# A language-and-state trunk on one core: modulation weights by 256 features a load, the last block's prompt windows first, and its output projection in two column parts

## The chip, the cores and the metric

The kernel runs on one core of a Trainium2 chip. The metric is device microseconds of one execution; three executions took 3923.26, 3939.91 and 3950.05 us, median 3939.91. One further execution was profiled and took 3942.07 us. The engines are TensorE (PE in the profile, its weight loads apart as PEld), VectorE (DVE), ScalarE (ACT), GpSimd (POOL) and SyncE (SP), whose queue issues most DMAs in order.

## The reference, cut to what matters

One inference step of a two-layer trunk over 1152 tokens of 1024 features: a prompt of 1024 tokens and eight samples of 16 tokens. Layer 0 is an RWKV-7 time mixing, layer 1 a band attention; each is followed by a SwiGLU feed-forward block.

```
mod = silu(c) @ w_ada[l] + b_ada[l]           # (rows, 6 * 1024): shift, scale, gate, twice
h = rms_norm(x) * (1 + scale) + shift
... r, w, k, v, a, g = projections of mixes of h and its previous row
s = s * w_t + (s a_t) b_t + v_t k_t           # the state, 64 x 64 per head, token by token
y_t = s r_t
out = (norm(y) + bonus) * g @ w_o             # output projection
x = x + gate * out
x = x + gate_f * swiglu(h_f)                  # h_f from rms_norm(x), modulated
```

c has nine rows: one for the prompt and one for each sample. `silu(c) @ w` over both layers and the shared keys and values has 14336 output features; this product is the modulation.

## The kernel before

The tokens are cut into three blocks of 384 columns (features stand on the partitions). Blocks 0 and 1 are prompt; in block 2 columns 0 to 255 are prompt and 256 to 383 are the samples. A float32 gemm is three products in a faster float32 form, with each operand split in a high and a low part: `split` lets ScalarE copy (L255) and VectorE subtract (L256), `mm3` issues the products (all matmuls have line L139).

**Modulation.** `ada_steps` (L195) is a generator over units of 512 output features; there are 28. A unit has four loads of 512 KB. Before, a load holds two k tiles of 128 input features by 512 output features. The product with k tile 4h+q goes into PSUM rows 32q to 32q+31; the two halves h of a unit accumulate, and a yield stands between them. At the unit's end ScalarE copies the bank, four small matmuls add the four row groups and transpose, and VectorE adds the bias into `mod`. Other code advances the generator: `step` (L190) in `proj_h` (units 0 to 3, into tiles of the window pool), in `proj_v` of block 2 (L631), in `layer0a` for what is left of units 4 to 11, and in `begin` (L1334) of the first feed-forward block's down projection for units 12 to 27. In `layer0a`'s last part the loads go into the ring of tiles called `raw`, which has two buffers there and serves the weights of the output projection (`wunit`, L245) too; in the down projection they go into tiles called `h`.

**Windows.** The recurrence runs in nine windows of 128 columns, each in two halves of eight heads (hf 0 and 1), so that a unit 2w+hf stands for one window and half. `windows` (L1083) prepares a unit (`win_prep`: reads, Gram products G, transposes), runs its states (`win_state`) and, beside the next unit's run, closes the one before (`win_post`, which writes `yg`). Units 12 and 13 are window 6, units 14 and 15 window 7; both are prompt columns of block 2, and a half's window 7 needs its state from window 6. Units 16 and 17 are window 8, the samples, whose states come from the input.

**Output projection.** `outproj` (L1114) reads `yg` of a block (`mr`, split into 16 `mx` tiles), then for each of eight features loads and splits a weight of `rw_o`, runs 24 products, adds the gated residual (`residual`, L1104), writes `x1` and sums squares; at the end it writes the inverse norm `rr`. The feed-forward block's first token half (tokens 0 to 511) needs blocks 0 and 1 only, its second half needs block 2.

**What sets the order.** `alternate(a, b, m, n)` (L1056) takes m steps of one generator, then n of the other; so the program order is a mix of windows, modulation and projections. The framework's scheduler then orders each engine's instructions, with waits where data or a buffer is not ready; each engine, and SP's queue, runs its list in order. In `layer0a` (L1140) windows 6 to 8 run in the order 12 13 16 14 15 17, five steps to two of `early`: what is left of the modulation units, then `outproj(0)` and `outproj(1)`. After the windows the pool is closed, `outproj(2)` follows, and `dense` starts the feed-forward block in the memory that was freed.

Of the kernel before, what the change touches and what calls it, by code (L numbers as in the profile page):

```python
# [11 lines left out]
ALU = mybir.AluOpType  # L12
# [5 lines left out]
TB = 384  # L18
# [59 lines left out]
def prep(i):  # L78
    i = {k: np.asarray(v) for k, v in i.items()}
    d = {}  # L80
# [57 lines left out]
def mm(nc, out, lhsT, rhs, start, stop):  # L138
    return nc.tensor.matmul(out, lhsT, rhs, start=start, stop=stop)  # L139


class Trunk:
# [52 lines left out]
    def ada_steps(self, units, tag="aux", bufs=1, tile=None):  # L195

        nc = self.nc
        for u in units:
            ps = self.bank(tag, bufs)
            for h in range(2):  # L200
                w = [(tile or self.rawtile)() for _ in range(2)]
                for i in range(2):
                    nc.sync.dma_start(w[i][:, :1024], self.a["wada"][u, 2 * h + i])
# [12 lines left out]
            nc.vector.tensor_tensor(self.mod[:, u * 4:u * 4 + 4, :], pv, bv, ALU.add)  # L216
            yield
# [69 lines left out]
    def sq_done(self, st):  # L287

        w = st.acc.shape[-1]
        if w == TB:  # L290
            ss = self.bank("aux", 1)[:, :TB]
            parts = [(ss, 0, TB)]
# [100 lines left out]
    def proj_h(self, b):  # L393
# [15 lines left out]
        for f in range(8):  # L409
            x = hb[:, f]  # L410
            if b == 0:
                if f % 4 == 0:
                    self.step(4)
                nc.vector.tensor_scalar(self.A0[f], self.mod[:, 8 + f, :], 1.0, self.P("nm0", f), ALU.add, ALU.mult)
# [689 lines left out]
    def residual(self, n, f, gate, out, x, ps):  # L1104

        nc = self.nc
        nc.vector.scalar_tensor_tensor(out[:, :n], ps[:, :n], self.mod[:, gate + f, 0:1], x[:, :n], ALU.mult, ALU.add)  # L1107
        if n < out.shape[-1]:
# [4 lines left out]

    def outproj(self, b):  # L1114

        nc, pp = self.nc, self.pp
        cols = slice(b * TB, (b + 1) * TB)
        hi, lo = [], []
        for f in range(8):
            h, l = self.mtile(), self.mtile()  # L1120
            t = self.mraw()
            nc.sync.dma_start(t, self.yg[b][:, f, :])
            self.split(h, l, t)
            hi.append(h)
            lo.append(l)
        st = self.sq_open()
        for f in range(8):
            W = self.wunit(pp, self.a["rw_o"][f])
            pz = self.bank("acc", 2)
            self.gemm(pz[:, :TB], W, hi, lo)  # L1130
            x = self.ev("rr")
            nc.sync.dma_start(x, self.a["x"][b][:, f, :])
            o = self.ev("e0")
            self.residual(256 if b == 2 else TB, f, 16, o, x, pz[:, :TB])
            nc.sync.dma_start(self.x1[:, f, cols], o)
            self.sq_add(st, o)
            yield
        nc.sync.dma_start(self.rr[:, cols], self.sq_done(st))

    def layer0a(self, ctx):  # L1140
# [26 lines left out]
        for _ in self.outproj(2):  # L1167
            pass
# [150 lines left out]
    def ffn(self, l, B, W, part1, xsrc, dst, done):  # L1319
# [14 lines left out]
        def begin(p):  # L1334
# [6 lines left out]
            W[p] = [self.halves(self.a[f"wd{l}"][f]) for f in (2 * p, 2 * p + 1)]  # L1341
            self.step(3)

# [567 lines left out]
```

## Time and profile before

| what | us |
|---|---|
| median of three executions | 3939.91 |
| profiled execution, its span | 3942.07, 3940.1 |
| PE busy over the span | 3559.0 (90%) |
| VectorE, ScalarE, GpSimd busy | 2265.0, 1574.5, 712.4 |
| mean granted PE clock | 0.929 of full |
| first and last modulation load of the windows' end | 954.8 to 1077.4 |
| first matmul of `outproj(2)` | 1334.74 |
| first product of the feed-forward block | about 1394 |

The parts of a page: busy shares by engine, the span in 40 slices, DMA queues, the chain of work that ended last, and groups of instructions by line. A row of a group reads: line, engine, operation, out<-in, shape, count | busy us, mean ns of one | idle us before them, with what ended it. Rows of the timeline and of the chain begin with the start and the length in us. A float32 matmul that is not in the faster form shows as two records. Each engine's busy time is a union over its own instructions, and matmuls are pipelined, so the distance from start to start says more than a record's length.

### The profile page before, as it was taken

What the parts mean: (1) busy time and instruction counts of PE and PEld (TensorE: products, weight loads), DVE (VectorE), ACT (ScalarE), POOL (GpSimd) and SP (SyncE); (2) the same over time, 40 slices, a digit from 0 to 9 for tenths busy, and PEclk for the clock granted to TensorE, in tenths of its full rate; (3) what the DMA queues carried; (4) which work ended last, traced back from release to release, by engine and by line L of the source; (5) the groups of instructions that cost most, each with busy time, mean ns of one, the idle gap of its engine ahead of it and who ended that gap; (6) DMA issues with size and microseconds to landing.
All of it is one profiled execution on the core that took longest, in us unless ns stands there. A gap on an engine that the chain in (4) does not pass through costs nothing.

```text
span 3940.1 us, 71465 instructions
## 1 busy us (share of the span) xinstructions
PE 3559.0 (90%) x28172; PEld 3107.7 (79%) x28172; DVE 2265.0 (57%) x4238; ACT 1574.5 (40%) x2967; POOL 712.4 (18%) x635
## 2 busy tenths in 40 slices
PE   6878988888798789999999999888889799999999
PEld 4766776776386579999877778777777789999998
DVE  5475575474355665555456752466676665455567
ACT  5554565363233343333311253455554443333310
POOL 0110110020000254545100210100000265454000
PEclk8888998799689689999999999999999899999999
DMA  6785675667665322222654313255464422222522
GB/s 214 210 243 155 181 232 168 170 186 215 186 167 163 100 90 78 74 76 72 228 183 164 133 60 102 79 169 153 143 195 155 154 70 75 75 73 93 170 79 74
DMA packets 434720, 552.27 MB, mean 140 GB/s; under 512 B 128336, under 2 KB 300496, under 8 KB 429904
## 3 DMA queue, kind: packets, MB, share of 16 engines
q1 hardware_dynamic: 380240, 528.82, 43.0%
q10 hardware_dynamic: 54144, 18.89, 2.1%
q8 instruction: 222, 3.64, 0.4%
q14 instruction: 114, 0.93, 0.1%
HBM read 413.44 MB, written 134.12 MB: 139 GB/s over the span
## 4 chain that ended last, share of the span: by engine, by line
PE 61%; DMA 6%; DVE 5%; ACT 3%; POOL 2%; issue 1%; SPq 0%; ACTq 0%; DVEq 0%; POOLq 0%
PE S L139 31%; PE PT L139 15%; PE acc L139 7%; PE st L139 2%; PE O L139 2%; DVE h L256 1%; PE PT L1737 1%; PE aux L139 1%; PE Y L139 1%; PE G L139 1%; DMA raw<-in_wada 1%; ACT pts L1738 1%; DMA h<-qT 0%; DMA h<-out_kT 0%; DMA h<-in_wq 0%
## 5 line engine op out<-in xcount | busy, mean ns | idle before, releaser
L139 PE MATMUL S<-h,w 128*128 128x320 f32 (+1 forms) x4944 | 695.5, 300 | 16.1 <-DVE h L256 3.4
L139 PEld LDWEIGHTS S<-h,w 128*128 128x128 f32 x4944 | 674.6, 192 | 24.2 <-DVE h L256 7.8
L139 PE MATMUL acc<-mx,whi 128*128 128x384 f32 x1728 | 525.6, 383 | 49.2 <-ACT mx L255 20.2
L139 PE MATMUL S<-h,wh 128*128 128x320 f32 (+1 forms) x2844 | 532.6, 338 | 14.5 <-DVE h L1107 8.1
L139 PEld LDWEIGHTS S<-h,wh 128*128 128x128 f32 x2844 | 457.3, 190 | 83.4 <-DVE h L1363 15.8
L139 PEld LDWEIGHTS acc<-mx,whi 128*128 128x128 f32 x1728 | 355.7, 214 | 77.6 <-ACT mx L255 23.3
L255 ACT ACTIVATE w<-rq 128x512 fp32r<-128x512 f32 x308 | 191.9, 629 | 503.3 <-PE S L139 200.5
L256 DVE TENSOR_TENSOR w<-rq,w 128x512 fp32r<-128x512 f32 x308 | 268.3, 875 | 198.4 <-ACT w L255 196.9
L139 PE MATMUL PT<-h,w 128*128 128x320 f32 (+1 forms) x2448 | 353.4, 299 | 15.1 <-ACT w L255 6.9
L139 PEld LDWEIGHTS PT<-h,w 128*128 128x128 f32 x2448 | 336.0, 192 | 18.9 <-ACT w L255 7.3
L139 PE MATMUL acc<-mx,wlo 128*128 128x384 f32 x864 | 325.7, 377 | 2.4 <-DVE wlo L256 2.4
L139 PE MATMUL PT<-h,wh 128*128 128x320 f32 (+1 forms) x1428 | 286.1, 344 | 7.6 <-DVE wh L256 4.7
L1296 POOL TENSOR_TENSOR t<-t,t 128x576 f32<-128x576 f32 (+1 forms) x132 | 214.5, 1625 | 413.5 <-ACT t L1303 295.7
L139 PEld LDWEIGHTS PT<-h,wh 128*128 128x128 f32 x1428 | 234.3, 190 | 42.9 <-DVE h L1363 6.9
L139 PEld LDWEIGHTS acc<-mx,wlo 128*128 128x128 f32 x864 | 184.0, 213 | 10.0 <-DVE wlo L256 3.7
L256 DVE TENSOR_TENSOR wlo<-raw,whi 128x1024 fp32r<-128x1024 f32 x108 | 136.7, 1267 | 94.7 <-ACT whi L255 93.5
L255 ACT ACTIVATE wh<-rq 128x512 fp32r<-128x512 f32 x124 | 75.0, 626 | 259.6 <-PE S L139 156.2
L256 DVE TENSOR_TENSOR h<-h,h 128x1024 fp32r<-128x1024 f32 (+4 forms) x112 | 123.3, 1115 | 83.0 <-ACT h L255 67.8
L255 ACT ACTIVATE h<-h 128x1024 fp32r<-128x1024 f32 (+4 forms) x112 | 103.1, 934 | 157.5 <-DMA h<-sd 105.7
L1296 DVE TENSOR_TENSOR t<-S,t 128x576 f32<-128x576 f32 (+1 forms) x116 | 86.5, 745 | 135.5 <-PE S L139 135.5
L1363 DVE TENSOR_TENSOR h<-h,S 128x640 f32<-128x640 f32 (+1 forms) x150 | 112.0, 751 | 83.0 <-PE S L139 82.6
L255 ACT ACTIVATE whi<-raw 128x1024 fp32r<-128x1024 f32 x108 | 113.5, 1053 | 104.5 <-PE acc L139 78.9
(424 smaller groups left out, 5758.5 us busy)
## 6 DMA issues: line engine op xcount, KB each, us to landing
h<-in_wada SPq DMA_DIRECT2D x64, 512.0 KB, 5.8
rq<-in_wg SPq DMA_DIRECT2D x88, 256.0 KB, 2.6
rq<-in_wu SPq DMA_DIRECT2D x88, 256.0 KB, 2.6
rq<-in_wd SPq DMA_DIRECT2D x88, 256.0 KB, 2.9
raw<-in_wada SPq DMA_DIRECT2D x32, 512.0 KB, 4.5
kc<-in_ck SPq DMA_DIRECT2D x16, 1024.0 KB, 5.0
vc<-in_cv SPq DMA_DIRECT2D x16, 1024.0 KB, 5.7
sd<-t SPq DMA_DIRECT2D x88, 160.0 KB, 1.9
```

The costliest lines, as they stand in the source:

```text
L139: return nc.tensor.matmul(out, lhsT, rhs, start=start, stop=stop)
L255: self.nc.scalar.activation(hi, x, AF.Copy)
L256: self.nc.vector.tensor_tensor(lo, x, hi, ALU.subtract)
L1296: eng.tensor_tensor(out, x, y, ALU.add)
L1363: nc.vector.tensor_tensor(y, y, d, ALU.add)
L1737: nc.tensor.transpose(pt[:, j * 128:(j + 1) * 128], P[:, j * 128:(j + 1) * 128], self.C("ident"))
L1738: nc.scalar.activation(pts[:, 0:nk * 128], pt[:, 0:nk * 128], AF.Copy)
```

## The change

Four things change.

1. The modulation weights are laid out so that a load has four k tiles by 256 output features. Each load now feeds the four row groups at once with products of 256 columns; the generator yields after each load, four times a unit. The callers' step counts follow: 8 for 4 in `proj_h`, one at each feature instead of each second one in `proj_v`, 7 for 3 in `begin`.
2. The windows' last part runs units 12 13 14 15 first, one step to one of a second mix, in which modulation steps and steps of `outproj(0)` and `outproj(1)` take turns one to one.
3. Units 16 and 17 follow, three steps to one of `outproj(2, 0, 256)`, the prompt columns of the last block.
4. After the windows only `outproj(2, 256, 384)` is left. Weights of `rw_o` are thus loaded and split 8 times more.

```diff
-    d["wada"] = np.ascontiguousarray(wa.reshape(4, 2, 128, 28, 512).transpose(3, 0, 2, 1, 4)).reshape(28, 4, 128, 1024)
+    d["wada"] = np.ascontiguousarray(wa.reshape(2, 4, 128, 28, 2, 256).transpose(3, 4, 0, 2, 1, 5)).reshape(28, 4, 128, 1024)
...
-            for h in range(2):
-                w = [(tile or self.rawtile)() for _ in range(2)]
-                for i in range(2):
-                    nc.sync.dma_start(w[i][:, :1024], self.a["wada"][u, 2 * h + i])
+            for i in range(4):
+                w = (tile or self.rawtile)()
+                nc.sync.dma_start(w[:, :1024], self.a["wada"][u, i])
+                c = slice(i // 2 * 256, i // 2 * 256 + 256)
                 for q in range(4):
-                    mm(nc, ps[32 * q:32 * q + 32, :], self.scT[:, 4 * h + q, :], w[q // 2][:, q % 2 * 512:q % 2 * 512 + 512],
-                       h == 0, h == 1)
-                if h == 0:
+                    mm(nc, ps[32 * q:32 * q + 32, c], self.scT[:, i % 2 * 4 + q, :], w[:, q * 256:q * 256 + 256], i % 2 == 0, i % 2 == 1)
+                if i < 3:
                     yield
...
-            if b == 2 and f % 2:
+            if b == 2:
                 self.step(1)
...
-    def outproj(self, b):
+    def outproj(self, b, c0=0, c1=TB):
...
-            self.residual(256 if b == 2 else TB, f, 16, o, x, pz[:, :TB])
+            x = self.ev("rr")[:, :w]
+            nc.sync.dma_start(x, self.a["x"][b][:, f, c0:c1])
+            o = self.ev("e0")[:, :w]
+            self.residual(0 if b == 2 and c0 else w, f, 16, o, x, pz)
...
+        def ada():
+            while next(self.ada, StopIteration) is not StopIteration:
+                yield
+
         def early():
-            for _ in range(16):
-                if next(self.ada, StopIteration) is StopIteration:
-                    break
-                yield
             for b in range(2):
                 yield from self.outproj(b)
-        for _ in self.alternate(self.windows([divmod(int(x), 2) for x in '12 13 16 14 15 17'.split()]), early(), 5, 2):
+        units = lambda t: self.windows([divmod(int(x), 2) for x in t.split()])
+        for _ in self.alternate(units("12 13 14 15"), self.alternate(ada(), early()), 1, 1):
+            pass
+        for _ in self.alternate(units("16 17"), self.outproj(2, 0, 256), 3, 1):
             pass
         cw.close()
-        for _ in self.outproj(2):
+        for _ in self.outproj(2, 256, 384):
             pass
...
-            self.step(3)
+            self.step(7)
```

What the scheduler makes of it is seen in the engines' lists. In the rows below `raw`, `h`, `acc`, `aux`, `st` are tiles (the number tells buffers' uses apart), `in_wada` the modulation weights, `in_rw_o` the output projection's weights. First SP's queue in the windows' last part, before; `pa`, `bn` are reads of the windows:

```order
L1017 DMA bn_11433<-sp_bn_95 128x512
L203 DMA raw_11501<-in_wada 128x1024
L203 DMA raw_11508<-in_wada 128x1024
L746 DMA pa_10754<-sp_kk_89 128x512
L746 DMA pa_10754<-sp_b_90 128x512
L203 DMA raw_11509<-in_wada 128x1024
L203 DMA raw_11672<-in_wada 128x1024
L203 DMA raw_11673<-in_wada 128x1024
```

Nine modulation loads stand in a row there, and four loads of `in_rw_o` follow. The same place now; `rr` and `mr` are reads of the projection, `x` its writes, `UV` and `XL` reads of the windows:

```order
L202 DMA raw_11432<-in_wada 128x1024
L825 DMA UV_11340<-sp_v_107 64x256 x2
L785 DMA XL_11281<-sp_kk_89 64x512
L786 DMA XL_11281<-sp_kk_89 64x512
L1136 DMA x_108<-e_1861_11275 128x384
L791 DMA XL_11281<-sp_r_92 128x512
L825 DMA UV_11340<-sp_v_107 64x256 x2
L247 DMA raw_11461<-in_rw_o 128x1024
L1133 DMA rr_11492<-in_x 128x384
L202 DMA raw_11511<-in_wada 128x1024
L1136 DMA x_108<-e_1888_11410 128x384
L1133 DMA rr_11559<-in_x 128x384
```

Loads of the two kinds take turns. Some 13 of the 16 features of the first two blocks' projections stand on PE before unit 12's first state product; before, less than one did. The last eight of the 24 modulation loads now come after the last projection weight of these two blocks.

Second PE in the down projection of the first feed-forward block, before; `PT` and `S` are the banks of the down projection, `acc` with `scT` is the modulation:

```order
L139 MATMUL acc_19307<-h_19308,scT 32x512 x2
L139 MATMUL PT_19368<-h_19248,wh_19267 128x512
L139 MATMUL PT_19368<-h_19249,wh_19267 128x512
L139 MATMUL PT_19368<-h_19248,wh_19268 128x512
L139 MATMUL PT_19368<-h_19248,wh_19279 128x512
L139 MATMUL PT_19368<-h_19249,wh_19279 128x512
L139 MATMUL PT_19368<-h_19248,wh_19280 128x512
L139 MATMUL acc_19307<-h_19309,scT 32x512 x2
```

A half unit's four products stand in two places, as its two loads land. The same part now:

```order
L139 MATMUL acc_19772<-h_19779,scT 32x256 x4
L139 MATMUL S_19851<-h_19705,wh_19724 128x512
L139 MATMUL S_19851<-h_19706,wh_19724 128x512
L139 MATMUL S_19851<-h_19705,wh_19725 128x512
L139 MATMUL acc_19772<-h_19785,scT 32x256 x4
```

Four products of 256 columns stand together, for most loads. Counted over the whole part, with at most four products to a group, there were 51 groups and are 72.

Third PE at the windows' end, before: `um` belongs to the sample unit's states, `acc` with `mx` to `outproj(2)`:

```order
L139 MATMUL st_12671<-um_12672,BKT_12354 64x256
L139 MATMUL st_12671<-um_12675,BKT_12354 64x256
L139 MATMUL st_12682<-um_12683,BKT_12354 64x256
L139 MATMUL st_12862<-y_12860,cst 128x512
L139 MATMUL st_12682<-um_12686,BKT_12354 64x256
L139 MATMUL st_12865<-y_12860,cst 128x512
L139 MATMUL acc_13313<-mx_13283,whi_13309 128x384
L139 MATMUL acc_13353<-mx_13283,whi_13349 128x384
```

All 192 products of the last block's projection come after the last unit. Now, in the first sample unit:

```order
L139 MATMUL acc_13319<-mx_12807,whi_13315 128x256
L139 MATMUL st_12918<-um_12919,BKT_12630 64x256
L139 MATMUL acc_13319<-mx_12808,whi_13315 128x256
L139 MATMUL acc_13319<-mx_12807,wlo_13316 128x256
L139 MATMUL acc_13319<-mx_12813,whi_13315 128x256
L139 MATMUL acc_13319<-mx_12814,whi_13315 128x256
L139 MATMUL st_12918<-um_12922,BKT_12630 64x256
L139 MATMUL acc_13319<-mx_12813,wlo_13316 128x256
```

The 192 products of 256 columns stand between the sample units' products, most of them under unit 16; 24 of the 192 products of 128 columns stand between unit 17's last ones, and 168 follow.

More of the change, by code (lines that the diff above doesn't have):

```diff
@@ L289, in sq_done @@
         w = st.acc.shape[-1]
-        if w == TB:
-            ss = self.bank("aux", 1)[:, :TB]
-            parts = [(ss, 0, TB)]
+        if w <= TB:
+            ss = self.bank("aux", 1)[:, :w]
+            parts = [(ss, 0, w)]
         else:
@@ L412, in proj_h @@
                 if f % 4 == 0:
-                    self.step(4)
+                    self.step(8)
                 nc.vector.tensor_scalar(self.A0[f], self.mod[:, 8 + f, :], 1.0, self.P("nm0", f), ALU.add, ALU.mult)
@@ L1106, in residual @@
         nc = self.nc
-        nc.vector.scalar_tensor_tensor(out[:, :n], ps[:, :n], self.mod[:, gate + f, 0:1], x[:, :n], ALU.mult, ALU.add)
+        if n:
+            nc.vector.scalar_tensor_tensor(out[:, :n], ps[:, :n], self.mod[:, gate + f, 0:1], x[:, :n], ALU.mult, ALU.add)
         if n < out.shape[-1]:
@@ L1112, in residual @@
             nc.vector.tensor_tensor(out[:, n:], t, x[:, n:], ALU.add)
-    def outproj(self, b):
+    def outproj(self, b, c0=0, c1=TB):
         nc, pp = self.nc, self.pp
-        cols = slice(b * TB, (b + 1) * TB)
+        w = c1 - c0
+        cols = slice(b * TB + c0, b * TB + c1)
         hi, lo = [], []
         for f in range(8):
-            h, l = self.mtile(), self.mtile()
-            t = self.mraw()
-            nc.sync.dma_start(t, self.yg[b][:, f, :])
+            h, l = self.mtile(w), self.mtile(w)
+            t = self.mraw()[:, :w]
+            nc.sync.dma_start(t, self.yg[b][:, f, c0:c1])
             self.split(h, l, t)
@@ L1128, in outproj @@
             W = self.wunit(pp, self.a["rw_o"][f])
[L1129 to L1133, printed above, removed]
-            self.residual(256 if b == 2 else TB, f, 16, o, x, pz[:, :TB])
+            pz = self.bank("acc", 2)[:, :w]
+            self.gemm(pz, W, hi, lo)
+            x = self.ev("rr")[:, :w]
+            nc.sync.dma_start(x, self.a["x"][b][:, f, c0:c1])
+            o = self.ev("e0")[:, :w]
+            self.residual(0 if b == 2 and c0 else w, f, 16, o, x, pz)
             nc.sync.dma_start(self.x1[:, f, cols], o)
```

## The prediction, made before the result was known

> **What bounds the kernel now.** I read the page's busy shares first.
>
> ```profile
> span 3940.1 us, 71465 instructions
> PE   6878988888798789999999999888889799999999
> PEclk8888998799689689999999999999999899999999
> ```
>
> Each digit is 98.5 us. TensorE (PE) is busy nearly everywhere, and its granted clock falls in slices 10 and 13 (about 985 to 1084 us and 1280 to 1379 us). Both lie where the change works: the first layer's last windows and output projections. A table by stretch gives the stages of that part, and last the down projection of the first feed-forward block (columns: stretch, length, then busy us of PE, weight loads, VectorE (DVE), ScalarE (ACT), GpSimd (POOL), then clock, DMA share, GB/s).
>
> ```profile
> 948.00:1098.00 150.00, 113.17 (x1526) 71.49 (x1523) 59.96 (x178) 33.08 (x71) 3.80 (x3) 0.66 0.72 206
> 1098.00:1166.00 68.00, 62.30 (x633) 54.22 (x633) 43.21 (x97) 25.25 (x45) 3.02 (x1) 0.95 0.62 170
> 1166.00:1250.00 84.00, 82.63 (x785) 64.72 (x783) 49.92 (x110) 25.19 (x43) 1.26 (x1) 0.94 0.56 162
> 1250.00:1334.00 84.00, 63.12 (x692) 42.87 (x691) 33.54 (x85) 18.02 (x35) 4.03 (x3) 0.77 0.28 84
> 1334.00:1394.00 60.00, 40.95 (x170) 36.66 (x171) 48.00 (x90) 31.92 (x64) 20.50 (x16) 0.73 0.44 146
> 1890.00:2220.00 330.00, 329.52 (x1909) 261.97 (x1909) 182.94 (x286) 73.89 (x103) 5.13 (x4) 1.00 0.56 196
> ```
>
> Row one is the modulation stretch: PE idles 36.8 of 150 us and runs at 0.66 of its clock. Rows two and three are full. In row four the last windows wait on themselves (20.9 us idle). Row five is the last block's projection, with VectorE at 80%. In the last row PE is the bound, so whatever is taken off PE there comes off the time. The groups, the SyncE (SP) queue and the chain of waits name the cause in row one:
>
> ```profile
> L139 PE MATMUL aux<-raw,scT 128*32 128x512 f32 x96 | 35.2, 928 | 17.7 <-DMA raw<-in_wada 14.7 <-DVE mod L216 2.6 <-issue 0.4
> 954.80 1.31 SPq L203 DMA_DIRECT2D raw<-in_wada  x2
> 1044.27 33.44 SPq L203 DMA_DIRECT2D raw<-in_wada  x9
> 1082.96 0.33 SPq L248 DMA_DIRECT2D raw<-in_rw_o  x1
> 1014.13 5.79 DMA raw<-in_wada
> 1023.19 5.49 DMA raw<-in_wada
> ```
>
> The modulation matmuls take 35.2 us and 17.7 us of idle time before them. Their 24 loads run through two buffers, and the first projection weight follows only at 1082.96. Until then no gemm is there to fill PE.
>
> **The change part by part.** I take the terms against the profiled execution's 3942.07 us (its span plus 2 us); the median of the runs shown is 3939.91, 2.2 us lower.
>
> *One modulation group.* Four products of 32 output rows run side by side in PE, each in two passes:
>
> ```profile
> 1913.34 1.92 PE L139 MATMUL acc<-h,scT 128*32 128x512 f32 x16
> 1924.54 1.05 PE L139 MATMUL acc<-h,scT 128*32 128x512 f32 x4
> L139 PE MATMUL acc<-h,scT 128*32 128x512 f32 x256 | 52.4, 602 | 0.5 <-DMA h<-in_wada 0.5
> ```
>
> Two products alone (x4) take 1.05 us, twice four products (x16) 1.92: so two more passes cost 0.87, one pass of 512 columns 0.435, and 0.18 is the pipeline's end. A product that runs alone or in a pair costs as much as four. That is what a load of two k tiles makes of them: 52.4 / 1.03 is 51 groups for 128 products. Now one load carries four products of 256 columns: an estimated 2 x 0.218 + 0.18 = 0.62 us a group at full clock.
>
> *Down projection.* The order has 72 such groups (64 loads, a few still split). 72 x 0.6 = 43 us against 52.4: **-9 us**, on the path since PE is full. If the pipeline's end hides behind the next matmul it is -12. The steps go from six loads a pair of features to seven; PE waited 0.5 us for them, so I cost that at nothing.
> The page "TensorE: Matmul & The Clock Gate" of the Trainium skill (Part 3, Packing small matmuls — row/col tiling) says that a weight load overlaps running matmuls only where its row group differs. Here all four products use all rows. By that rule each pass would also pay its weight load, which halving the columns makes worse. The x16 row speaks against it: nothing but streaming fits into 0.435 us a pass.
>
> *Modulation stretch, own matmuls.* 24 loads at 0.62 to 0.62 / 0.66 = 0.94 us make 15 to 22.5 us; at 0.7 I take 17 for 35.2: **-18 us** (-13 to -20).
>
> *Modulation stretch, waits.* Now a projection weight is loaded between two modulation loads, and the order puts some 13 of the 16 features of the first two blocks' projection here. Of the 36.8 us idle I take away the 17.7 before modulation matmuls and 3 more: **-21 us** (0 to -33: nothing, or only 4 us left).
>
> *Modulation stretch, clock.* The other PE work is 113.2 - 35.2 = 78 us at 0.66. With gemms in between I take 0.85: 61 us, **-17 us** (0 to -26, at full clock). The 13 features cost here what they cost later; I count them as moved.
>
> *Last block's projection in two parts.* A gemm's spacing comes from starts:
>
> ```profile
> 1100.39 0.51 PE L139 MATMUL acc<-mx,whi 128*128 128x384 f32 x2
> 1100.92 0.51 PE L139 MATMUL acc<-mx,whi 128*128 128x384 f32 x2
> 1897.25 6.56 PE L139 MATMUL S<-h,w 128*128 128x256 f32 x48
> 1903.65 3.36 PE L139 MATMUL PT<-h,w 128*128 128x256 f32 x24
> 1919.42 0.96 PE L139 MATMUL acc<-cst,h 128*128 128x16 f32 x8
> ```
>
> Three products of 384 columns stand in 0.53 us, 0.177 each; 48 of 256 in 6.40, 0.133 each; products of 16 columns still take 0.10 to 0.12, which is the weights' floor. So the 192 products of 384 (34 us) become 192 of 256 (25.6 us) and 192 of 128 (19 to 25.6 us). The first set now stands under the sample windows. If that stretch is full, as rows two and three are, it adds **+26 us**; if it fills the idle 20.9 us of row four, nothing; at 0.77 of the clock, +33. Eight more weight loads and splits come with it:
>
> ```profile
> raw<-in_rw_o SPq DMA_DIRECT2D x24, 512.0 KB, 4.4
> L255 ACT ACTIVATE whi<-raw 128x1024 fp32r<-128x1024 f32 x108 | 113.5, 1053 | 104.5 <-PE acc L139 78.9
> L256 DVE TENSOR_TENSOR wlo<-raw,whi 128x1024 fp32r<-128x1024 f32 x108 | 136.7, 1267 | 94.7 <-ACT whi L255 93.5
> ```
>
> That is 8.4 us of ACT and 10.1 us of DVE, under stretches where both are at most 60% busy: nothing on the path; without that cover 10 us.
>
> *The tail after the last window* (60 us, row five):
>
> ```profile
> L139 PE MATMUL acc<-mx,whi 128*128 128x384 f32 x112 | 35.9, 408 | 21.6 <-ACT mx L255 12.6 <-DVE e L1111 8.3 <-DVE h L256 0.7
> L1107 DVE SCALAR_TENSOR_TENSOR e<-acc,mod,rr 128x256 f32<-128x256 f32 x8 | 3.8, 480 | 2.5 <-PE acc L139 2.4
> L285 DVE TENSOR_TENSOR sqa<-sqa,kk 128x384 f32<-128x384 f32 x7 | 4.1, 589 | 1.7 <-ACT kk L284 1.7
> 1334.74 1.33 PE L139 MATMUL acc<-mx,whi 128*128 128x384 f32 x3 [9.78 <-ACT mx L255]
> ```
>
> PE waits for VectorE's and ScalarE's work, which the first feed-forward part shares. VectorE loses the 3.8 us of L1107, two thirds of 4.1 and about one us of splits: 48.0 becomes 40.5. With the 9.8 us that the last window's write and read take before the first gemm, the tail is about 50 us: **-10 us** (+6, if the eight weights come late, to -20). PE's 128-column products, 25.6 / 0.73 = 35 us, fit into that.
> By the page "TensorE: Matmul & The Clock Gate" (Back-to-back issue gap) a stream of pairs of weight load and 128-column matmul goes at 81 ns. Then these 192 take an estimated 15.6 us; no row here has that form, and since VectorE ends the tail the sum would stay.
>
> *The added wait.* The same 9.8 us of write and read now also stand between the last prompt unit and the prompt columns of the last block. Four reads of them wait at the head of SP's in-order queue, and behind them stand the writes of the sample states and projection weights; on PE the first gemms wait in line before the sample unit's state products. Ahead of them PE has that unit's first products, so I cost it at nothing; without that cover it is 10 us.
>
> *Projection of the values, last block.* The same eight loads, one a feature instead of two every second:
>
> ```profile
> L139 PE MATMUL aux<-raw,scT 128*32 128x512 f32 x32 | 8.1, 719 | 0.7 <-DMA raw<-in_wada 0.7
> ```
>
> 8 x 0.62 = 5 us for 8.1: **-3 us** (0 at worst). The 16 loads at the start stay the same bytes, and PE waits for them: nothing.
>
> *Sum:* -9 - 18 - 21 - 17 + 26 - 10 - 3 = -52 us; 3942 - 52 = **3890 us**.
>
> **The rivals.** A difference of 1%, 39 us, is about what a measurement here tells from no change.
>
> *It fills better.* The 256-column products and the moved features go into idle time: +26 becomes 0, waits go by 28 instead of 21, the clock to 0.9 (-21 instead of -17). 3890 - 37 = 3853 us. For it: row four's idle 20.9 us at 84 GB/s. Against: its windows are a chain, and the order puts the products mostly under the first sample unit, not the last.
>
> *The waits move.* With 13 features gone ahead, the four prompt units run with little to fill and wait on their own steps, as in row four. Then -21 and -17 are paid back: 3890 + 38 = 3928 us. For it: 1250 to 1334 shows what windows without gemms look like. Against: rows two and three have 25 us each of other PE work in 68 and 84 us, so the chain leaves room.
>
> *The weight load shows in each pass.* 96 groups of two passes pay the 0.108 us more: 3890 + 21 = 3911 us. Its row is here, and the x16 row speaks against it:
>
> ```profile
> L139 PEld LDWEIGHTS acc<-h,scT 128*32 128x32 f32 x256 | 8.2, 108 | 15.7 <-issue 13.6 <-DVE h L1107 0.7 <-DVE h L1363 0.7
> ```
>
> *Slower: the two raw buffers.* Modulation and projection weights now take turns in one ring of two. A projection weight is held through landing (4.4), split (1.05 + 1.27) and until a pair of split buffers is free; while it waits, the modulation load behind it on SP's in-order queue waits too, and behind that the windows' loads. From 954.8 to 1083.0 the ring served 24 loads and 6 result rows: 30 holds, 8.5 us each. Now 47 holds (24 loads, 6 result rows, 17 projection weights) must pass in about 210 us, so 8.9 us are allowed. Each us beyond costs 47 / 2 = 23.5 us. From 12.7 us a hold the kernel is over 1% slower; at 13 us it takes 3986 us. For it: the ring is near its limit. Against: 4.4 + 1.05 + 1.27 is 6.7 us, and a modulation load needs no split.
>
> **How the numbers follow.** Forecast 0.49, better filling 0.20, moved waits 0.18, weight loads 0.05, ring 0.08. The forecast's own range is 3865 to 3915, about three quarters of it below 3901. Faster by over 1%: 0.37 + 0.20 = 0.57; slower by over 1%: the ring, 0.08; the rest, 0.35, within 1%. The range takes in better filling (3853, with 10 us more for the lower bounds of the modulation terms) and moved waits: 3843 to 3930. It leaves out the ring and the outer ends.
>
> **What would show it.** Modulation matmuls in the down projection at 40 to 45 us instead of 52.4, in the modulation stretch at 15 to 23 instead of 35.2; PE clock there over 0.8 and idle under 20 us; the last window's end about 35 us earlier, the first feed-forward product 40 earlier, with 50 us between them. If loads of in_wada or in_rw_o end PE's waits for more than 25 us together, the ring is the story; if ScalarE and VectorE steps of the windows do (xs, UV, S), the waits have moved. I am wrong if the stretch from 948 us to the first feed-forward product is not 20 us shorter.

## The result and the profile after

The changed kernel takes 3968.10 us (median of 7 runs) for 3939.64 before: ratio 1.0072, 95% interval 1.0047 to 1.0097. Timed once more beside a later group of experiments it gave 1.0063 (1.0048 to 1.0078). So it is slower, by 25 to 28 us, where 52 us faster was forecast. Its profiled execution took 3959.5 us, 17.4 more than that of before and 9 less than its own median. Here is how its page begins:

```profile
span 3957.6 us, 72834 instructions
PE   6878998888887889999999999888889789999999
PEclk8888898798887769999999999999999889999999
```

The clock's low slice 10, from 985 us, is gone (8 for 6), but slices 11 to 14, from 1090 us on, read 8 7 7 6 where they read 8 9 6 8. The table by stretch: the first three rows are cut as in the prediction, the fourth is the tail after the last window, the fifth the down projection.

```profile
948.00:1098.00 150.00, 123.67 (x1451) 98.22 (x1452) 78.50 (x187) 47.32 (x88) 5.74 (x3) 0.81 0.75 218
1098.00:1166.00 68.00, 63.83 (x733) 52.54 (x732) 41.46 (x105) 20.40 (x40) 1.09 (x1) 0.89 0.59 157
1166.00:1250.00 84.00, 61.73 (x678) 47.35 (x679) 30.28 (x74) 23.98 (x47) 2.71 (x3) 0.76 0.54 149
1353.00:1416.00 63.00, 39.21 (x171) 37.10 (x170) 44.99 (x90) 29.42 (x66) 17.32 (x16) 0.52 0.36 113
1935.00:2247.00 312.00, 312.00 (x2110) 259.55 (x2109) 181.95 (x298) 67.40 (x94) 4.04 (x3) 1.00 0.53 190
```

The modulation stretch did become what the prediction said: the clock went from 0.66 to 0.81 and idle time from 37 to 26 us. Row three has it back: 1166 to 1250 was full at 0.94 and now has 22 us idle at 0.76. The sum over the whole part, from the write of unit 8 (the last unit to close while the projections run) to the first feed-forward product, before and after:

```profile
938.80:1394.00 455.20, 371.18 (x3918) 277.10 (x3917) 237.54 (x563) 137.23 (x265) 34.49 (x25) 0.79 0.56 162
```

```profile
933.00:1416.20 483.20, 395.17 (x4213) 314.10 (x4212) 253.23 (x588) 148.74 (x293) 30.84 (x25) 0.78 0.57 163
```

I split each into PE's work at full clock (busy time by clock), what the clock adds to it, and idle time: 293 + 78 + 84 us before, 308 + 87 + 88 after. (The clock is the mean of the whole stretch, so the first two are good to some 4 us.) Nothing of the 84 us idle and the 78 us of clock was saved, though PE's modulation matmuls in this part halved (first row; the second row is the down projection's):

```profile
L139 PE MATMUL aux<-raw,scT 128*32 128x256 f32 x192 | 16.3, 421 | 7.8 <-DMA raw<-in_wada 6.1 <-DVE kk L306 1.7
L139 PE MATMUL acc<-h,scT 128*32 128x256 f32 x512 | 40.6, 387 | 0.0
```

Before, these two read 35.2 and 52.4 us. The down projection's stretch is 5 us shorter (312 for 317). In this pair of profiles the part is 28 us longer and begins 6 us sooner, so the first feed-forward product starts 22 us later; all that follows takes 5 us less, which makes the 17.

### The profile page after: what moved, and what is told of

Its sections match the earlier page's. It is cut to its first block, busy times and chain, and to the rows that moved or that the text cites. A ratio compares the mean times of both kernels' runs of the same rounds, so it can differ in the third digit from the quotient of the medians.

```text
span 3957.6 us, 72834 instructions
## 1 busy us (share of the span) xinstructions
PE 3572.2 (90%) x28814; PEld 3153.8 (80%) x28814; DVE 2284.7 (58%) x4263; ACT 1586.3 (40%) x2994; POOL 708.6 (18%) x635
## 5 line engine op out<-in xcount | busy, mean ns | idle before, releaser
L139 PE MATMUL acc<-mx,whi 128*128 128x384 f32 (+2 forms) x1856 | 558.1, 382 | 63.9 <-ACT mx L254 31.1
L139 PEld LDWEIGHTS acc<-mx,whi 128*128 128x128 f32 x1856 | 386.3, 223 | 99.7 <-ACT mx L254 36.1
L139 PE MATMUL acc<-mx,wlo 128*128 128x384 f32 (+2 forms) x928 | 347.0, 375 | 7.1 <-DVE wlo L255 7.0
L255 DVE TENSOR_TENSOR wlo<-raw,whi 128x1024 fp32r<-128x1024 f32 x116 | 146.1, 1262 | 127.3 <-ACT whi L254 126.3
L139 PEld LDWEIGHTS acc<-mx,wlo 128*128 128x128 f32 x928 | 205.0, 221 | 15.9 <-DVE wlo L255 9.1
L254 ACT ACTIVATE whi<-raw 128x1024 fp32r<-128x1024 f32 x116 | 121.8, 1053 | 143.2 <-PE acc L139 82.2
```

The source lines that it names most:

```text
L254: self.nc.scalar.activation(hi, x, AF.Copy)
L255: self.nc.vector.tensor_tensor(lo, x, hi, ALU.subtract)
```

## The experiments

Theory and rivals at the start: *order* (the new order moves waits into the prompt units and wins nothing), *division* (the two column parts add work), *layout* (small loads disturb the projections).

### One part at a time

`e1_layout` is the kernel before with the new layout alone.

```diff
+                self.step(1)          # early(): two steps of one load each, for one of two
                 yield
```

> The kernel before with part one of the change alone: modulation loads of four k tiles by 256 features, one step a load, step counts 8, 1 and 7, and two steps a yield in the windows' last part, so that modulation still goes ahead of the projections at the old rate. Window order and the undivided last projection as before. Theory 'order' (the loss comes from how the windows' last part is put in order): the layout by itself is a gain, 5 us in the down projection (the profile after shows 312 us for the stretch that was 317) and 5 to 20 us in the modulation stretch, ratio 0.994 to 0.998. Theory 'division' (the loss is the work that the two column parts add): the same, 0.994 to 0.998. Theory 'layout' (loads one at a time disturb the projections and windows, whose unit 11 closed 13 us later after): 1.000 or more.

Measured: 0.9967 (0.9956 to 0.9979), 13 us faster. The theory *layout* falls. Its profiled execution is 20 us shorter than that of before: 8 of them behind the first feed-forward product, 4 between the write of unit 8 and it, and 8 ahead of unit 8, where kernels with the new layout and the same work lie up to 17 us apart (922.5 to 939.9), so that these are not read.

`e2_order` is the changed kernel with the old layout.

```diff
-    wa.reshape(2, 4, 128, 28, 2, 256) ...   # and ada_steps, step counts as before
+    wa.reshape(4, 2, 128, 28, 512) ...
```

> The changed kernel with the old modulation layout (two k tiles by 512 features, two loads a step): order of the windows and division of the last projection as changed. Theory 'order': the time after plus what the layout had saved, 3942 + 25 to 50 us, ratio 1.007 to 1.013. Theory 'division': the same. Theory 'layout': 1.003 or less.

Measured: 1.0030 (1.0018 to 1.0042). All theories missed: -13 and +12 make -1, not the +25 to +28 of both. The new order costs more with the new layout than with the old.

`e3_whole` is the changed kernel without the division.

```diff
...
-        for _ in self.alternate(units("16 17"), self.outproj(2, 0, 256), 3, 1):
+        for _ in units("16 17"):
             pass
         cw.close()
-        for _ in self.outproj(2, 256, 384):
+        for _ in self.outproj(2):
```

> The changed kernel with the last block's projection undivided: units 16 and 17 run with nothing beside them, then all 384 columns. Theory 'order': the prompt units 13 to 15 still run with modulation matmuls alone beside them (30 us idle there), and the sample units now have no cover, so it stays at or above the kernel before, ratio 1.000 to 1.008. Theory 'division': the divided products cost 41 us of PE time more than the undivided ones (44.1 + 31.3 for 34.6 us), so without them it falls below the kernel before: 0.993 to 0.998, although 256-column products then leave the sample units.

Measured: 1.0030 (1.0019 to 1.0042). The division costs 13 to 17 us, and the rest of the change stands 12 us above the kernel before, although the layout by itself takes 13 off. So *order* and *division* each hold a part.

`e4_mix` has the new layout, the old unit order, and modulation and features one to one.

```diff
...
+        for _ in self.alternate(units("12 13 16 14 15 17"), self.alternate(ada(), early()), 5, 4):
```

> New layout, old window order 12 13 16 14 15 17 at five steps to four of the mix, modulation steps and projection features one to one, last projection undivided. Theory 'order': gemms come between the modulation loads without the prompt units being bared, so the idle time of the stretch up to 1083 us falls from 36.8 to under 25 us and the time goes below that of the layout alone, ratio 0.990 to 0.997. Theory 'division': the mix as such is worth nothing, same as the layout alone, 0.994 to 0.998. If the mix itself moves waits into units 14, 15 and 17, it is 1.000 or more.

Measured: 1.0003 (0.9987 to 1.0019), 14 us slower than the layout alone. The mix that was to fill the modulation stretch costs time.

### Pace, ring and layout against order

With the new layout a turn of the mix issues one modulation load where it issued two. `f1_pair` gives it two:

```diff
             while next(self.ada, StopIteration) is not StopIteration:
+                self.step(1)
                 yield
```

> The changed kernel, with two modulation loads instead of one at each turn of the mix with projection features, so that modulation keeps the pace that it had with two loads a step. Layout alone gave 0.9967 (-13 us), the new order and division with the old layout 1.003 (+12 us); together they should give -1 us and give +28. Theory 'pace': the missing 29 us come from the halved pace, which leaves modulation matmuls as the only work beside the prompt units 13 to 15 (30 us idle there); with the pace restored the sum holds, ratio 0.998 to 1.002. Theory 'ring' (two raw buffers that both kinds of weights share are the limit): the pace changes nothing, 1.005 or more. Theory 'division' (divided products alone): 1.005 or more as well.

Measured: 1.0004 (0.9991 to 1.0017), 23 to 27 us better than the changed kernel, as *pace* says. The edit also changes the turns in the ring and PE's list, so it shows what two loads a turn are worth, not by which of these.

`f2_ring3`: `(2, 2, 2)` becomes `(3, 2, 2)` in the changed kernel.

> The changed kernel with three raw buffers instead of two in the windows' last part. Theory 'ring': the waits of the SyncE queue for a raw buffer (15.4 + 8.1 + 8.0 + 7.9 us in the first 180 us) go, and with them 15 to 25 us: 1.001 to 1.004. Theory 'pace': PE waited only 3.1 us for modulation weights and 3.8 for the split of projection weights there, so at most 7 us: 1.0055 to 1.0075.

Measured: 1.0017 (0.9998 to 1.0037), 18 to 22 us better than the changed kernel. So the ring has a share. But the scheduler also writes another PE list for three buffers, so this run doesn't tell the waits for a buffer from the order that follows from it.

`f3_oldwhole`: `e2_order` with the last projection undivided, as in `e3_whole`.

> Old modulation layout, new order of the windows' last part (prompt units first, modulation and features one to one), last projection undivided: the changed order alone. The same with the division took 1.003. Theory 'pace': with two loads a step the order alone costs nothing, and the division costs what it costs with the new layout (1.0072 to 1.003, 16 us): 0.997 to 1.001. If the order itself costs with either layout: 1.002 or more, and the division is then worth less than 5 us here.

Measured: 1.0009 (0.9994 to 1.0023). With two loads a turn the order costs about nothing (4 us, 6 either way), the division 8 us (7 either way).

`f4_lay3`: `e1_layout` with three raw buffers.

> The layout alone (which took 0.9967), with three raw buffers instead of two in the windows' last part. PE waits 15.5 us there for modulation weights, at a DMA share of 0.78 and 217 GB/s. If the ring of two limits these loads, a third buffer takes 8 to 15 us off: 0.993 to 0.9947. If the transfers themselves are the limit, nothing: 0.9955 to 0.998.

Measured: 1.0003 (0.9988 to 1.0018), *slower* than with two, which neither side expected. The third buffer did speed the loads: from the first to the last 100.5 us instead of 110.4. But PE's list then has 151 projection products ahead of unit 12's second chain of state products (36 with two buffers), and unit 12 closes 17 us later.

### The tail, the division, the order of loads

`g0_after` is the changed kernel again.

> The changed kernel again, as it is, timed beside the next three, so that all stand on the same chip and the same runs of the kernel before. 1.0072 by seven runs; every theory expects 1.005 to 1.009.

Measured: 1.0063 (1.0048 to 1.0078).

`g1_pairwhole`: `f1_pair` with the last projection undivided.

> The changed kernel with two modulation loads at each turn of the mix (which took it from 1.0072 to 1.0004) and with the last projection undivided. Theory 'division': the divided products are still 16 us dearer here, as between 1.0072 and 1.003, so 0.995 to 0.998. If the pace and the division pay for the same thing (bare windows), the two gains don't add: 0.9985 to 1.0015.

Measured: 0.9997 (0.9985 to 1.0009). The division is worth 3 us here, 7 either way. That it is cheaper here than the 13 to 17 us above isn't clear of the noise; by the profiles (table below) it is 9 us here and 14 there.

`g2_tail256` makes the tail's products 256 columns wide, by computing 128 columns twice:

```diff
-            self.residual(0 if b == 2 and c0 else w, f, 16, o, x, pz)
+            self.residual(128 if b == 2 and c0 else w, f, 16, o, x, pz)
...
-        for _ in self.outproj(2, 256, 384):
+        for _ in self.outproj(2, 128, 384):
```

> The changed kernel, but the part of the last projection after the windows runs on columns 128 to 383 instead of 256 to 383: 128 prompt columns are computed a second time, to the same values, so that its 192 products have 256 columns. Theory 'width': 128-column products don't keep the granted clock up (64.9 us in one piece at 0.50 in the profile after), 256-column products do: clock of the tail 0.7 or more, so twice the columns take no longer (192 x 0.133 = 25.6 us at full clock, 35 at 0.73, for 44.1 measured), ratio 1.002 to 1.008. Theory 'waits': the clock falls because PE waits for VectorE and ScalarE between features, so it stays near 0.5, the products take 51 us and VectorE has more to do: 10 us or more slower than the changed kernel, 1.009 to 1.014.

Measured: 1.0067 (1.0050 to 1.0084): twice the columns for nothing, as *width* says, with the tail's clock at 0.67, just short of the 0.7 that it gave. The tail's products by group, first in the changed kernel:

```profile
L139 PE MATMUL acc<-mx,whi 128*128 128x128 f32 x112 | 35.8, 418 | 15.3 <-ACT mx L254 10.9 <-DVE e L1111 3.7 <-DVE mx L255 0.7
```

and with 256 columns, with the tail's stretch:

```profile
L139 PE MATMUL acc<-mx,whi 128*128 128x256 f32 x112 | 30.2, 369 | 26.4 <-DVE e L1111 13.5 <-ACT mx L254 11.9 <-DVE mx L255 0.9
1365.00:1426.00 61.00, 33.08 (x171) 30.20 (x171) 45.21 (x90) 30.31 (x64) 21.08 (x16) 0.67 0.42 134
```

112 products of 128 columns keep PE busy for 35.8 us; 112 of 384 columns took 35.9 before. Twice the width takes less, at 0.67 of the clock instead of 0.52, and then PE waits for VectorE.

`g3_first` is the changed kernel with modulation first, as before, and all else as changed.

```diff
-        for _ in self.alternate(units("12 13 14 15"), self.alternate(ada(), early()), 1, 1):
+        for _ in self.alternate(units("12 13 14 15"), chain(ada(), early()), 1, 1):
```

> The changed kernel with all modulation steps of the windows' last part ahead of the projection features, as in the kernel before, instead of one to one; prompt units first and the divided projection as changed. In the ring of two raw buffers the projection weights then come last, and PE's list has projection products under all four prompt units (86 + 19 + 22 + 28 + 12 of them after the second chain of unit 14, where the changed kernel has 21 after modulation products alone). Theory 'pace' (bare prompt units cost the time): what the mix lost comes back, 0.996 to 1.000. Theory 'division' (the divided products alone): 1.005 or more.

Measured: 1.0020 (1.0005 to 1.0035): 17 to 20 us of the loss go with the mix, but it ends above the range that *pace* gave.

### What sets the time of this part

`i1_firstwhole` is `g3_first` undivided. It differs from `e1_layout` by the unit order and by how the program is mixed: units 12 to 15 share one mix with modulation and projections, and 16 and 17 follow alone.

> The layout alone (0.9967) with one thing more: the units run in the order 12 13 14 15 16 17, prompt units first, instead of 12 13 16 14 15 17. Modulation still goes ahead of the projections, the last projection is undivided. With the last projection divided as well this took 1.0020. Theory 'filler': the two sample units now stand together at the end with nothing beside them (55 and 31 us bare in the changed order, 47 and 20 us in the old one), which costs 15 to 25 us; the division then adds little: 1.000 to 1.003. Theory 'division': the order is free, and the 21 us between 0.9967 and 1.0020 are the price of the divided products: 0.996 to 0.998.

Measured: 0.9966 (0.9945 to 0.9988), the same as the layout alone. The unit order, mixed like this, is free; *filler* falls. Against `g3_first` the division costs 21 us here, 10 either way; by the profiles it is 13.

`i2_third` leaves out two thirds of the products in the changed kernel's first two output projections:

```diff
+            if b < 2:
+                for k in range(8):
+                    mm(nc, pz, W[0][:, k * 128:k * 128 + 128], hi[k], k == 0, k == 7)
+            else:
+                self.gemm(pz, W, hi, lo)
```

> The changed kernel with two of the three products of each pair left out in the output projections of blocks 0 and 1 (only high part times high part is computed; the output is less exact by that): 256 of 384 products of 384 columns fewer, 61 us of PE's 93 us on them in the profile after. Theory 'chain' (units run at the pace of their own steps, and PE's idle time and low clock are what a chain of small products leaves, whatever is put beside it): less than 25 us come off, ratio 1.000 to 1.006, and idle time and clock loss between unit 8 and the feed-forward block grow by 30 us or more. Theory 'PE' (PE's work sets the pace): 45 to 61 us come off, 0.991 to 0.995.

Measured: 1.0007 (0.9995 to 1.0019), 22 to 26 us less than the changed kernel. Its part from unit 8 to the feed-forward block:

```profile
921.80:1391.40 469.60, 368.17 (x3960) 282.79 (x3958) 251.03 (x588) 147.61 (x293) 30.26 (x25) 0.71 0.57 168
```

261 + 107 + 101 us, for 308 + 87 + 88: of 47 us less work at full clock 20 came back as a lower clock and 13 as idle time, and the part is 14 us shorter. That is the *chain* case, at the edge of its "less than 25 us": by the medians about half of what is taken off PE comes off the time, by this pair of profiles less than a third.

`h1_move` takes 8 of the 24 modulation loads of the windows' part into the down projection:

```diff
-            self.ada = self.ada_steps(range(4, 12))
+            self.ada = self.ada_steps(range(4, 10))
...
-        self.ada = self.ada_steps(range(12, 28), "acc", 1) if l == 0 else iter(())
+        self.ada = self.ada_steps(range(10, 28), "acc", 1) if l == 0 else iter(())
```

> The layout alone (0.9967) with modulation units 10 and 11, the gate of the first feed-forward block, taken out of the windows' last part and put ahead of units 12 to 27 in the down projection: 8 of 24 loads fewer in the ring of two, 8 more where PE is the bound. Theory 'stretch' (a load there costs its turn in the ring, 115 us / 24 = 4.8 us): 38 us less there and 8 x 0.6 = 5 us more in the down projection, 0.987 to 0.992. Theory 'chain': the projection's features move up into a lump before unit 12 (202 products in a row in PE's list), and units 14, 15 and 17 are left bare, so what is saved is paid back: 0.996 to 1.000.

Measured: 0.9978 (0.9965 to 0.9991), no better than 0.9967. The loads end 28 us sooner, 82.5 us after the first; 202 projection products then stand ahead of unit 12's second chain (36 with the layout alone; 93 of them in one row), and unit 12 closes 22 us later. *Stretch* falls.

### All of them in one table

Every unit's close is the start of its write of `yg`. The first column of times is from the first modulation load of the windows' part to the close of unit 12, the second to that of unit 17, the third from there to the first feed-forward product, all in us of the profiled execution. "1:1" is one modulation load to one feature, "2:1" two.

| kernel | modulation, last projection | ratio | unit 12 | unit 17 | tail |
|---|---|---|---|---|---|
| before | old layout, first, whole, old unit order | 1 | 196.6 | 374.6 | 64.6 |
| e1_layout | first, whole, old unit order | 0.9967 | 181.8 | 361.7 | 66.3 |
| i1_firstwhole | first, whole | 0.9966 | 185.5 | 369.8 | 65.6 |
| h1_move | first (16 loads), whole, old unit order | 0.9978 | 203.5 | 367.0 | 65.4 |
| f4_lay3 | first, ring of 3, whole, old unit order | 1.0003 | 198.6 | 371.6 | 66.1 |
| g1_pairwhole | 2:1, whole | 0.9997 | 203.0 | 378.3 | 66.0 |
| e4_mix | 1:1, whole, old unit order | 1.0003 | 214.3 | 370.8 | 66.6 |
| e3_whole | 1:1, whole | 1.0030 | 207.5 | 382.5 | 64.3 |
| g3_first | first, divided | 1.0020 | 183.3 | 389.7 | 58.4 |
| f1_pair | 2:1, divided | 1.0004 | 206.1 | 394.6 | 58.7 |
| f2_ring3 | 1:1, ring of 3, divided | 1.0017 | 203.7 | 396.6 | 58.4 |
| after | 1:1, divided | 1.0072 | 207.8 | 402.1 | 58.8 |
| g0_after | the same, again | 1.0063 | 211.4 | 408.9 | 58.9 |
| g2_tail256 | 1:1, divided, tail of 256 columns | 1.0067 | 210.8 | 402.0 | 61.3 |
| i2_third | 1:1, divided, a third of the early products | 1.0007 | 198.5 | 388.4 | 58.4 |
| e2_order | old layout, 1:1 (two loads a turn), divided | 1.0030 | 204.9 | 388.5 | 59.0 |
| f3_oldwhole | old layout, 1:1 (two loads a turn), whole | 1.0009 | 206.0 | 376.9 | 64.3 |

Along one path from before to after the steps are: layout -13 us, unit order 0, mix 1:1 +25 (0.9966 to 1.0030), division +13 to +17 (1.0030 to 1.0063 or 1.0072), together +25 to +29. Each step's interval is 5 to 11 us either way. On other paths the mix costs 14 us (old unit order) or 17 to 20 (divided), the division 3 (2:1) or 21 (modulation first). Single profiled executions lie up to 15 us off their medians, and the two of the changed kernel differ by 4 and 7 us in the first two columns, so small differences there are not read.

What the columns show, the mix first: with the new layout, whatever puts projection features ahead of unit 12 (1:1, 2:1, a third buffer, fewer loads) closes it 17 to 33 us later than `e1_layout` does. Units 13 to 15, barer for it, win back less: 89 us for 102 in `e3_whole` against `i1_firstwhole`. The features' products on PE are only a part of this. `i2_third` has 112 of them ahead of unit 12's second chain where the changed kernel has 348, and PE's work at full clock up to unit 12's close is 104 us, no more than with modulation first (101 to 107); yet unit 12 closes 13 to 17 us later than there and only 9 to 13 sooner than in the changed kernel. What else of a feature delays the unit (its splits and residuals on ScalarE and VectorE, its turns in the ring and in SP's queue) no run separates.

Then the division: unit 17 closes 16 to 20 us later (1:1, 2:1, first), and the tail gives 5 to 7 back, so 9 to 14 us remain in each of the three pairs; PE's work at full clock is some 15 us more in each.

The ratio of windows to the rest moves nothing in `e1_layout`: with four to one, three to one or eight to three instead of five to two (forms that were not timed) the scheduler writes the same lists for PE and SP. So what is compared in the table is the turns in the ring of raw buffers, modulation against features, with the ring's size, the units' order, the layout and the division.

The version that beats both kernels is the layout alone, 0.9967; the next to it, 0.9966, can't be told from it.

## Why the prediction was wrong

**Right: the layout's own matmuls.** Modulation in the down projection: forecast 43 us, measured 40.6, 0.56 us a group for the 0.62 estimated. In the modulation stretch -18, measured 35.2 to 16.3. As time it is less: `e1_layout` closes unit 12 15 us sooner after the first modulation load than before, reaches the feed-forward block 11 us sooner, and takes 8 us less behind that, for 9 forecast; in the pair before and after these 8 are 5. By the medians the layout alone is worth 13 us. The rival of weight loads shown in each pass falls with this row after the change:

```profile
1935.17 1.93 PE L139 MATMUL acc<-h,scT 128*32 128x256 f32 x32
```

Eight passes of 256 columns take as long as four of 512 did before (1.92 us): half the columns take half the time, which leaves no room for a weight load in each pass.

**The step that failed: "waits -21" and "clock -17".** I read idle time and a low clock in one stretch as losses that other work can fill, and counted the projection features as moved at no cost ("The 13 features cost here what they cost later; I count them as moved"). In that stretch they did shrink, by 10.5 us of idle time and to a clock of 0.81. But over the part idle time went from 84 to 88 us and the clock's share from 78 to 87: +13 us where -38 was forecast. The sign that the prediction named for itself came too: from 948 us to the first feed-forward product it is 468 us, not 20 less than the 446 of before. `i2_third` shows that this room was not free: of 47 us of work taken off PE, 33 came back as waiting and low clock. And the features that moved ahead of unit 12 made it late: it closes 22 to 26 us later after the first modulation load than in `i1_firstwhole`, of which `i2_third` puts 9 to 13 down to their products on PE. What makes up the rest stays open. The forecast charged moved work nothing where it went. These waits name the place, PE's longest between 1127 and 1260 us after the change:

```profile
PE Y L139 <- DVE UV L931: 4.9, 1, 4.9
PE G L139 <- issue: 4.0, 1, 4.0
PE st L139 <- ACT UV L932: 3.1, 1, 3.1
PE G L817 <- DVE XL L808: 3.0, 1, 3.0
PE aux L139 <- DMA raw<-in_wada: 3.0, 1, 3.0
```

```profile
1127.00:1260.00 133.00, 102.63 (x1249) 79.21 (x1247) 59.26 (x148) 36.81 (x72) 5.07 (x4) 0.82 0.55 146
```

The stretch has 30.4 us idle in 133, and most of the waits listed there (some 18 of 28 us) end with steps of the windows (UV, XL and the like), as the rival "the waits move" said. Its mechanism is seen, but its 3928 us is too low, by 31 for the profiled execution and 40 for the median: it paid back only what I had booked and let the other terms stand.

**Also wrong: the tail, -10.** It became 6 us shorter, and not for the reason given. I let VectorE end it and fitted PE's 128-column products in at 0.73 of the clock, 35 us. The clock stood at 0.50 in one piece of 64.9 us (from 1355.8), and the 192 products kept PE busy for 44 us; the 168 of them in the tail took 38.4, for 40.0 that 168 undivided ones had taken. (Before the change, too, 24 of the 192 run ahead of the last unit's close, between 1286 and 1297 us: not all of them come after it, as the section on the change has it.)

**Near in size, wrong in what it buys: the division, +26.** The 256-column products kept PE busy for 33 us, and unit 17 closes 16 to 20 us later with the division than without. I had set against that a full -10 from the tail; 5 to 7 came.

**The added wait, nothing or 10 us:** it is there, at half its price.

```profile
1262.82 0.80 PE L139 MATMUL acc<-mx,whi 128*128 128x256 f32 x2 [4.93 <-ACT mx L254]
```

**Projection of the values, -3:** nothing is seen of it. The first modulation load of the windows' part starts at 955.4 us, 954.8 before; over all profiles at 945 to 963 us with the new layout and at 948 to 955 with the old one.

**The ring of two,** forecast as 8.9 us a hold allowed and slower from 12.7: from the first modulation load to the first weight of the last block (955.4 to 1212.0) 24 loads, 6 result rows and 16 weights took 11.2 us a hold. By the price that this rival set (23.5 us for each us beyond 8.9) that is 54 us, so the forecast gave it too little weight; but a hold also lasts longer when PE is late (SP waited 8.0 and 5.8 us for modulation products to free a buffer), so 11.2 us doesn't show by itself that the ring was the limit. Two rows of the queue's waits up to 1127 us:

```profile
SPq L247 <- DVE wlo L255: 15.4, 5, 7.5
SPq L202 <- DMA raw<-in_rw_o: 8.1, 5, 2.7
```

The third buffer gave 18 to 22 us back in the changed kernel, and took 14 in the layout alone. PE itself waited only some 7 us for these weights up to 1127. How much of the gain is waiting for a buffer, and how much the other order of PE's list, stays open. Open, too, is whether the division costs less beside one mix (3 us, 7 either way) than beside another (21, 10 either way): the profiles give 9 and 13 us. No run changed the place of products in PE's list alone.

## What to carry to other kernels

Idle time and low clock beside a chain of small dependent steps need not be free room: before filling them, leave out some of the other work, as `i2_third` does, and see whether the time falls by as much. Work that is moved is to be charged where it lands, above all where it lands ahead of a chain; and, as `i2_third` shows, not for its products on PE alone. When a change has parts, time each alone: here the small one was worth 13 us, and the two that came with it cost 40.

## What was not expected of the hardware

*With products of 128 columns the clock stayed at half.* In all seven profiles of a tail with them (the changed kernel twice, `e2_order`, `f1_pair`, `f2_ring3`, `g3_first`, `i2_third`) the granted clock is 0.50 for one piece of 64.9 us. A product mostly started 0.21 us after the one before, and after the first wait (8.95 us in the changed kernel) no gap of PE was longer than 2.3 us. With 256 columns (`g2_tail256`) the clock went up and down between 0.50 and 1.00, although PE had longer gaps, up to 5.8 us, and the tail took about the same time (61 us for 59). The Trainium skill, "TensorE: Matmul & The Clock Gate" (Part 1, The HAM clock gate), says that the clock has two states, half and full, and is granted by windows of some 3.4 us; the records here agree, 0.50 and 1.00 alone, in pieces of a multiple of 3.4 us (64.9 is 19 of them). The Trainium skill's rule to have no idle gaps over about 3.4 us (same page, HAM oscillation) was not enough to bring the clock back here: after the first wait there were none, and the clock stayed down. The width is not the only thing that does this: where modulation goes first in the new layout, a piece of 78.5 us at 0.50 begins at 1018 to 1022 us (`e1_layout`, `i1_firstwhole`, `g3_first`), and before the change the longest there is 34.1 us.

*A third buffer made a kernel slower* (0.9967 to 1.0003), with its loads 10 us faster.
